# A two-layer hybrid block on one core: how eight PSUM banks are shared between score tiles and projections

## The chip, the cores and the metric

The kernel runs on one core of a Trainium2 chip. The metric is the device time of one execution in microseconds (us). The kernel before was timed three times: 2352.19, 2362.51 and 2359.31 us, median 2359.31 us. The profile was taken on a fourth execution of 2353.76 us, whose span from the first to the last instruction is 2352.0 us.

## The reference

Two blocks of two layers each work on 512 tokens of width 1024, all in fp32.

```python
# first block, twice
h = rms_norm(x, norm_g); proj = h @ w_in            # 14 pieces
y_nsa  = compressed + selected + window attention, gated   # 8 heads, causal, 512 keys
y_lru  = gated linear recurrence over a 4-tap convolution
y_conv = silu(layernorm(31-tap depthwise convolution)) @ w_pw2
x = x + concat(y * silu(z)) @ w_out
# second block, layer 0 then layer 1
x = x + mixer_ab(rms_norm(x))     # dense attention (a) and windowed attention with a sink (b), 8 heads each
x = x + cross_attention(x, mem)   # 4 heads, 256 memory tokens
x = x + swiglu(x)
x = x + mixer_cd(rms_norm(x))     # latent attention (c) and neighbourhood attention (d), 8 heads each
x = x + cross_attention(x, mem); x = x + swiglu(x); return rms_norm(x)
```

## The kernel before, in words

Activations lie transposed: eight tiles `X` of 128 channels by 512 tokens. A projection tile multiplies 128 output channels with all 512 tokens over eight tiles of `X`. Every operand of a projection is split in a high part and a low part, and each product is made by three matmuls (L410, L411, L412). So a projection tile (`dense_tile`, L443) is 24 matmuls into one PSUM bank, and VectorE or ScalarE then empties that bank. Weights come by DMA in chunks (`wr`), ScalarE makes the high part `wh` (L432), VectorE or GpSimd the low part `wl` (L365).

PSUM has eight banks. One letter each in `lay` (L301 to L305, read at L346) gives them to four uses: m projections, s scores, t transposes and statistics, o attention outputs. `lay` is `mmssstto` in the stages b (first block, both layers), a (mixer_ab) and c (mixer_cd), and `mmssttoo` in x (cross attention) and f (feed-forward). Within a letter a tile takes whichever bank of that letter is free.

Which letter a projection tile asks for is decided at L445 and L446: the letters in `spare` for the first tiles after a norm, then the letters in `dense` in turn, but only m while attention is under way (`quiet` is false from L728 until L777). The token-major projections (`tok_major`, L455) open four banks at once, by the letters in `tok`. The convolution of the first block also uses s: for each of its four channel tiles VectorE gathers 31 taps in an s bank (L895 to L899), at a low priority.

`attn` (L721) goes through pairs of query tiles. For each query tile it makes the scores of two heads, three matmuls each (L743), into two s banks; VectorE takes the row minimum (`mn`, L750 with a mask, L754 without), ScalarE the exponential into the SBUF tile `p` (L377), which frees the bank. One step later `attn_back` (L779) scales `p` (L372), transposes it on TensorE into a t bank (L798), copies it out on ScalarE (`ptt`, L805), and multiplies with the values into an o bank (L813). L745 sets which exponential a pair of score tiles has to come after:

```python
freed = len(self.exps) + nh - 1 - self.banks.count("s")
```

With two heads and three s banks that is the first exponential of the pair before; with four it is the second of the pair before that one.

The generators of a stage are stepped in the order of written strings (`FIRST`, `SECOND`, `CD_FIRST`, `CD_SECOND`), so that projections stand between the steps of attention. A scheduler then puts all instructions in order at build time, by priorities, dependences and free buffers. Each engine runs its list in that order on the chip.

Of the kernel before, what the change touches and what calls it, by code (L numbers as in the profile page):

```python
# [286 lines left out]
class Net:  # L287
# [10 lines left out]
    CD_FIRST = "0000iiiiA1rA111B2rB222C3C333D4D444D"  # L298
    CD_SECOND = "E5oE5o5F6oF6o6G7oG7o7HoH"
    CFG = {  # L300
        "b": dict(lay="mmssstto", spare="mmss", dense="m", tok="mmss", stat="t", ahead=1, pv=-200, sc="vvvv", cp=0, low=-4000, wp=0),  # L301
        "a": dict(lay="mmssstto", spare="msss", dense="ms", tok="ssmm", stat="t", ahead=1, pv=-200, sc="vvvv", cp=0, low=-4000, wp=0),
        "x": dict(lay="mmssttoo", spare="mmss", dense="ms", tok="mmss", stat="t", ahead=1, pv=-200, sc="avav", cp=0, low=-4000, wp=0),
        "f": dict(lay="mmssttoo", spare="mmss", dense="ms", tok="mmoo", stat="o", ahead=1, pv=-200, sc="avav", cp=0, low=-4000, wp=0),
        "c": dict(lay="mmssstto", spare="mmss", dense="m", tok="mmss", stat="t", ahead=1, pv=-200, sc="vvvv", cp=0, low=-4000, wp=0),  # L305
    }

    def __init__(self, tc, ctx, ap, pcols):
# [1324 lines left out]
```

## Time and profile before

| what | value |
|---|---|
| profiled execution, its span | 2353.76 us, 2352.0 us |
| runs, median | 2352.19 to 2362.51 us, 2359.31 us |
| TensorE busy | 2185.8 us, 93% |
| VectorE busy | 1464.4 us, 62% |
| ScalarE busy | 962.7 us, 41% |
| GpSimd busy | 451.4 us, 19% |
| mean granted TensorE clock | 0.971 |
| DMA | 194.73 MB, mean 83 GB/s |

Busy means that an instruction of the engine was under way. The clock is the share of full speed granted to TensorE: 1.0 is 2.4 GHz and 0.5 is 1.2 GHz. The stages lie roughly so, in us from the span's start: layer 0 of the first block up to 450 (its attention from 290), layer 1 to 885 (attention from 700), mixer_ab to 1145 (attention from 968), cross attention to 1210, feed-forward to 1600, mixer_cd to 1885, cross attention to 1960, feed-forward and the last norm to the end.

### The profile page before, as it was taken

What the parts mean: (1) busy time and instruction counts of PE and PEld (TensorE: products, weight loads), DVE (VectorE), ACT (ScalarE), POOL (GpSimd) and SP (SyncE); (2) the same over time, 40 slices, a digit from 0 to 9 for tenths busy, and PEclk for the clock granted to TensorE, in tenths of its full rate; (3) what the DMA queues carried; (4) which work ended last, traced back from release to release, by engine and by line L of the source; (5) the groups of instructions that cost most, each with busy time, mean ns of one, the idle gap of its engine ahead of it and who ended that gap; (6) DMA issues with size and microseconds to landing.
All of it is one profiled execution on the core that took longest, in us unless ns stands there. A gap on an engine that the chain in (4) does not pass through costs nothing.

```text
span 2352.0 us, 29320 instructions
## 1 busy us (share of the span) xinstructions
PE 2185.8 (93%) x11052; PEld 1731.6 (74%) x11052; DVE 1464.4 (62%) x2496; ACT 962.7 (41%) x1823; POOL 451.4 (19%) x452
## 2 busy tenths in 40 slices
PE   7999989998999989869999999999999899999998
PEld 5677856677777658546778888887767688888887
DVE  8997575499876564656665544454676655544444
ACT  4432365424235552455463322233377545322223
POOL 4434411343343133110211000001100102000002
PEclk9999999999999999989999999999999999999999
DMA  4343211133331112311323333332312132333332
GB/s 137 96 131 105 73 36 37 54 103 113 101 97 57 34 37 72 87 31 37 96 91 96 94 97 99 92 97 81 103 61 73 44 113 68 95 98 99 91 98 90
DMA packets 61436, 194.73 MB, mean 83 GB/s; under 512 B 8432, under 2 KB 10480, under 8 KB 61296
## 3 DMA queue, kind: packets, MB, share of 16 engines
q1 hardware_dynamic: 52848, 179.75, 25.0%
q10 hardware_dynamic: 8448, 13.12, 2.0%
q8 instruction: 87, 1.43, 0.3%
q14 instruction: 53, 0.43, 0.1%
HBM read 182.61 MB, written 2.10 MB: 79 GB/s over the span
## 4 chain that ended last, share of the span: by engine, by line
PE 68%; DVE 14%; DMA 7%; ACT 6%; issue 3%; POOL 2%; ACTq 1%; DVEq 0%; SPq 0%; POOLq 0%
PE ps_m L410 12%; PE ps_m L411 11%; PE ps_m L412 11%; PE ps_s L412 7%; PE ps_s L410 6%; PE ps_s L411 6%; DMA wr<-ws 4%; PE ps_s L743 4%; PE ps_o L813 3%; DVE ps_s L368 3%; PE ps_t L798 3%; ACT p L377 2%; DVE wl L365 1%; ACT wh L432 1%; ACT ptt L805 1%
## 5 line engine op out<-in xcount | busy, mean ns | idle before, releaser
L432 ACT CAST wh<-wr 128x1024 fp32r<-128x1024 f32 (+2 forms) x312 | 323.1, 1035 | 660.7 <-DMA wr<-ws 553.9
L365 DVE TENSOR_TENSOR wl<-wr,wh 128x1024 fp32r<-128x1024 f32 (+1 forms) x232 | 288.2, 1242 | 300.4 <-PE ps_m L411 140.4
L410 PE MATMUL ps_m<-xh,wh 128*128 128x512 f32 x1008 | 400.1, 397 | 17.5 <-ACT wh L432 7.9
L412 PE MATMUL ps_m<-xh,wl 128*128 128x512 f32 x1008 | 399.9, 397 | 4.0 <-POOL wl L365 2.8
L411 PE MATMUL ps_m<-xl,wh 128*128 128x512 f32 x1008 | 397.6, 394 | 2.8 <-DVE xl L368 2.8
L362 POOL TENSOR_TENSOR sq<-sq 128x512 f32<-128x512 f32 (+1 forms) x62 | 87.2, 1407 | 951.3 <-ACT sq L377 951.3
L365 POOL TENSOR_TENSOR wl<-wr,wh 128x1024 fp32r<-128x1024 f32 (+2 forms) x80 | 191.0, 2387 | 386.8 <-PE ps_m L411 220.1
L410 PEld LDWEIGHTS ps_m<-xh,wh 128*128 128x128 f32 x1008 | 191.1, 190 | 63.9 <-issue 10.3
L412 PEld LDWEIGHTS ps_m<-xh,wl 128*128 128x128 f32 x1008 | 190.7, 189 | 50.0 <-POOL wl L365 5.5
L411 PEld LDWEIGHTS ps_m<-xl,wh 128*128 128x128 f32 x1008 | 190.8, 189 | 46.5 <-DVE xl L368 4.8
L377 ACT ACTIVATE p<-ps_s,mn 128x512 f32<-128x512 f32 (+3 forms) x288 | 164.1, 576 | 78.7 <-DVE mn L750 40.9
L412 PE MATMUL ps_s<-xh,wl 128*128 128x512 f32 x480 | 188.4, 393 | 1.0 <-DVE wl L365 1.0
L410 PE MATMUL ps_s<-xh,wh 128*128 128x512 f32 x480 | 188.0, 392 | 0.0
L411 PE MATMUL ps_s<-xl,wh 128*128 128x512 f32 x480 | 187.7, 391 | 0.0
L368 DVE SCALAR_TENSOR_TENSOR ps_s<-up,params,ps_s 128x512 f32<-128x512 f32 x232 | 170.0, 750 | 2.6
L805 ACT COPY ptt<-ps_t 128x512 f32<-128x512 f32 (+3 forms) x288 | 129.2, 478 | 103.5 <-PE ps_t L798 101.4
L798 PE MATMUL ps_t<-consts,p 128*128 128x128 f32 x848 | 137.7, 294 | 23.0 <-ACT ptt L805 11.7
L798 PEld LDWEIGHTS ps_t<-consts,p 128*128 128x128 f32 x848 | 103.5, 148 | 60.8 <-ACT ptt L805 24.1
L362 DVE TENSOR_TENSOR X<-ps_m,X 128x512 f32<-128x512 f32 (+1 forms) x136 | 90.8, 671 | 58.7 <-PE ps_m L412 58.4
L412 PEld LDWEIGHTS ps_s<-xh,wl 128*128 128x128 f32 x480 | 90.7, 189 | 20.6 <-DVE wl L365 1.5
L411 PEld LDWEIGHTS ps_s<-xl,wh 128*128 128x128 f32 x480 | 90.6, 189 | 19.0
L410 PEld LDWEIGHTS ps_s<-xh,wh 128*128 128x128 f32 x480 | 90.6, 189 | 18.7 <-issue 0.2
(504 smaller groups left out, 4146.6 us busy)
## 6 DMA issues: line engine op xcount, KB each, us to landing
wr<-ws SPq DMA_DIRECT2D x318, 512.0 KB, 3.6
strip<-strips ACTq DMA_DIRECT2D x8, 480.0 KB, 4.6
wr<-ws SPq DMA_DIRECT2D x8, 384.0 KB, 3.1
X<-x SPq DMA_DIRECT2D x8, 256.0 KB, 4.8
mem<-mem SPq DMA_DIRECT2D x8, 256.0 KB, 3.0
wr<-ws SPq DMA_DIRECT2D x7, 256.0 KB, 2.7
tab<-tables SPq DMA_DIRECT2D x6, 256.0 KB, 2.8
out_dram<-ox SPq DMA_DIRECT2D x8, 128.0 KB, 1.7
```

The lines of the kernel that those rows point to most:

```text
L362: (eng or self.nc.vector).tensor_tensor(out=out, in0=a, in1=b, op=ALU.add)
L365: (eng or self.nc.vector).tensor_tensor(out=out, in0=a, in1=b, op=ALU.subtract)
L368: self.nc.vector.scalar_tensor_tensor(out=out, in0=a, scalar=s, in1=b, op0=op0, op1=op1)
L377: return self.nc.scalar.activation(out, in_, func, **k)
L410: mm(out, ah, bh, start=first, stop=False)
L411: mm(out, ah, bl, start=False, stop=False)
L412: return mm(out, al, bh, start=False, stop=last)
L432: nc.scalar.copy(wh[:, :n], wr[:, :n])
L743: run.append(lambda s=s, q=q, k=k, n=n: nc.tensor.matmul(s, q[:, sl], k[:, ks], start=n == 0, stop=n == np_ - 1))
L798: nc.tensor.transpose(t[:, j * P:(j + 1) * P], p[:, j * P:(j + 1) * P], self.con("ident"))
L805: nc.scalar.copy(dst, src)
L813: run.append(lambda n=n, j=j, a=a, b=b, hd=hd, t=t: nc.tensor.matmul(hd[2]()[:, (pr + a) * P:(pr + b) * P], hd[1](j), t[:, j, a * P:b * P] ...
```

## The change

Three of the five stages get another table of banks: b, a and c. In all three, one m bank becomes a fourth s bank. Projection tiles outside attention go to m and s in turn (b and c had m alone), the tiles after a norm go to one m and three s (`msss`), and the token-major projections to four s. The stages x and f are as they were.

```diff
-        "b": dict(lay="mmssstto", spare="mmss", dense="m", tok="mmss", stat="t", ...
-        "a": dict(lay="mmssstto", spare="msss", dense="ms", tok="ssmm", stat="t", ...
+        "b": dict(lay="msssstto", spare="msss", dense="ms", tok="ssss", stat="t", ...
+        "a": dict(lay="msssstto", spare="msss", dense="ms", tok="ssss", stat="t", ...
...
-        "c": dict(lay="mmssstto", spare="mmss", dense="m", tok="mmss", stat="t", ...
+        "c": dict(lay="msssstto", spare="msss", dense="ms", tok="ssss", stat="t", ...
```

The first place is TensorE's list in the dense attention of mixer_ab. Before, the rows are these (`ps_s` are scores, `ps_t` transposes, `ps_o` the product with the values):

```order
L798 MATMUL ps_t<-consts,p 128x128 x16
L743 MATMUL ps_s<-qh 128x512 x2
L743 MATMUL ps_s<-qh,ql 128x512 x2
L743 MATMUL ps_s<-ql,qh 128x512 x2
L813 MATMUL ps_o<-ptt,abv 64x256 x8
```

The changed program has these rows there:

```order
L813 MATMUL ps_o<-ptt,abv 64x256 x8
L798 MATMUL ps_t<-consts,p 128x128 x8
L743 MATMUL ps_s<-qh 128x512 x2
L743 MATMUL ps_s<-qh,ql 128x512 x2
L743 MATMUL ps_s<-ql,qh 128x512 x2
L798 MATMUL ps_t<-consts,p 128x128 x4
L743 MATMUL ps_s<-qh 128x512 x2
L743 MATMUL ps_s<-qh,ql 128x512 x2
L743 MATMUL ps_s<-ql,qh 128x512 x2
L798 MATMUL ps_t<-consts,p 128x128 x12
```

Sixteen transposes stood in one piece between two pairs of score tiles; now pairs of score tiles stand between pieces of eight, four and twelve transposes.

The second place is TensorE's list in the first block, layer 0, where the projections `zn` run beside the first attention (2617 and 2653 are two tiles of that projection). Before:

```order
L412 MATMUL ps_m_2617<-xh_133,wl_2621 128x512
L1157 MATMUL ps_t_2024<-consts_74,cs_2013 128x128 x2
L410 MATMUL ps_m_2617<-xh_137,wh_2620 128x512
L411 MATMUL ps_m_2617<-xl_138,wh_2620 128x512
L412 MATMUL ps_m_2617<-xh_137,wl_2621 128x512
L410 MATMUL ps_m_2653<-xh_109,wh_2656 128x512
L411 MATMUL ps_m_2653<-xl_110,wh_2656 128x512
```

Now:

```order
L412 MATMUL ps_m_2617<-xh_133,wl_2621 128x512
L410 MATMUL ps_m_2617<-xh_137,wh_2620 128x512
L411 MATMUL ps_m_2617<-xl_138,wh_2620 128x512
L412 MATMUL ps_m_2617<-xh_137,wl_2621 128x512
L410 MATMUL ps_m_2653<-xh_109,wh_2656 128x512
L411 MATMUL ps_m_2653<-xl_110,wh_2656 128x512
```

The two tiles follow each other in both lists. Before, they lie in the two m banks; now both lie in the only one, so that the first matmul of 2653 comes after VectorE has emptied 2617.

## Rows read from the trace of the kernel before

**Rows 1.** Engine busy times by stretch: PE, PEld, DVE, ACT, POOL, granted clock, DMA.

```profile
50.00:150.00 100.00, 91.37 (x415) 71.93 (x414) 99.77 (x130) 39.40 (x51) 43.10 (x30) 0.97 0.36 110
290.00:450.00 160.00, 138.62 (x807) 97.61 (x806) 102.14 (x274) 86.58 (x228) 31.16 (x24) 0.95 0.13 37
700.00:885.00 185.00, 166.59 (x933) 120.92 (x932) 113.85 (x288) 99.80 (x246) 54.03 (x37) 0.94 0.14 43
968.00:1045.00 77.00, 53.28 (x326) 32.95 (x326) 41.10 (x82) 40.81 (x95) 7.61 (x6) 0.89 0.10 26
1045.00:1145.00 100.00, 87.15 (x505) 63.10 (x506) 67.08 (x173) 56.60 (x150) 14.20 (x19) 0.93 0.17 51
1690.00:1860.00 170.00, 156.42 (x931) 113.32 (x930) 110.70 (x220) 114.47 (x247) 11.27 (x18) 1.00 0.19 58
2000.00:2300.00 300.00, 300.00 (x1313) 246.33 (x1312) 146.21 (x177) 82.04 (x94) 0.00 (x0) 1.00 0.32 95
```

**Rows 2.** TensorE's waits over the span: total us, times, longest us.

```profile
PE ps_s L743 <- ACT p L377: 33.4, 29, 5.3
PE ps_o L813 <- ACT ptt L805: 18.0, 23, 2.3
PE ps_m L410 <- DVE X L362: 14.8, 10, 3.5
PE ps_t L798 <- ACT ptt L805: 11.7, 26, 1.5
...
PE ps_t L798 <- DVE p L372: 8.7, 11, 1.6
```

**Rows 3.** The timeline of mixer_ab's attention: start us, us, engine, instruction, idle before.

```profile
1001.30 1.28 DVE L754 TENSOR_REDUCE mn<-ps_s 128x1 f32<-128x512 f32 x2
1001.39 1.14 PE L798 MATMUL ps_t<-consts,p 128*128 128x128 f32 x8 [0.59 <-ACT ptt L805]
...
1002.61 0.69 ACT L377 ACTIVATE p<-ps_s,mn 128x512 f32<-128x512 f32 x1
...
1003.29 0.68 ACT L377 ACTIVATE p<-ps_s,mn 128x512 f32<-128x512 f32 x1
1003.44 0.50 PE L743 MATMUL ps_s<-qh 64*128 64x512 f32 x2 [0.91 <-ACT p L377]
1003.78 0.40 PE L743 MATMUL ps_s<-qh,ql 64*128 64x512 f32 x2
```

**Rows 4.** The timeline where a projection waits longest for its bank.

```profile
1879.87 2.28 DVE L365 TENSOR_TENSOR wl<-wr,wh 128x1024 fp32r<-128x1024 f32 x1
1882.08 0.68 DVE L362 TENSOR_TENSOR X<-ps_m,X 128x512 f32<-128x512 f32 x1
...
1882.90 0.55 PE L410 MATMUL ps_m<-mh,wh 128*128 128x256 f32 x1 [3.50 <-DVE X L362]
```

**Rows 5.** The instructions that empty a projection's bank: ns min/median/max.

```profile
L368 DVE SCALAR_TENSOR_TENSOR z<-ps_m,rb x24: 677/690/694, 101.6 to 724.9; 128x512 f32<-128x512 f32 x24
```

**Rows 6.** TensorE's timeline in a projection beside attention.

```profile
255.03 0.39 PE L410 MATMUL ps_m<-xh,wh 128*128 128x512 f32 x1
255.26 0.39 PE L411 MATMUL ps_m<-xl,wh 128*128 128x512 f32 x1
```

**Rows 7.** The last convolution tap of each layer, and the first token-major matmuls.

```profile
215.78 0.75 DVE L368 SCALAR_TENSOR_TENSOR cy<-up,params,ps_s 128x512 f32<-128x512 f32 x1
...
220.23 0.50 PE L470 MATMUL ps_s<-wh,xh 128*128 128x280 f32 x2
...
648.89 0.75 DVE L368 SCALAR_TENSOR_TENSOR cy<-up,params,ps_s 128x512 f32<-128x512 f32 x1
...
650.82 0.50 PE L470 MATMUL ps_s<-wh,xh 128*128 128x280 f32 x2
```

More of the change, by code (lines that the diff above doesn't have):

```diff
@@ L300 @@
     CFG = {
-        "b": dict(lay="mmssstto", spare="mmss", dense="m", tok="mmss", stat="t", ahead=1, pv=-200, sc="vvvv", cp=0, low=-4000, wp=0),
-        "a": dict(lay="mmssstto", spare="msss", dense="ms", tok="ssmm", stat="t", ahead=1, pv=-200, sc="vvvv", cp=0, low=-4000, wp=0),
+        "b": dict(lay="msssstto", spare="msss", dense="ms", tok="ssss", stat="t", ahead=1, pv=-200, sc="vvvv", cp=0, low=-4000, wp=0),
+        "a": dict(lay="msssstto", spare="msss", dense="ms", tok="ssss", stat="t", ahead=1, pv=-200, sc="vvvv", cp=0, low=-4000, wp=0),
         "x": dict(lay="mmssttoo", spare="mmss", dense="ms", tok="mmss", stat="t", ahead=1, pv=-200, sc="avav", cp=0, low=-4000, wp=0),
         "f": dict(lay="mmssttoo", spare="mmss", dense="ms", tok="mmoo", stat="o", ahead=1, pv=-200, sc="avav", cp=0, low=-4000, wp=0),
-        "c": dict(lay="mmssstto", spare="mmss", dense="m", tok="mmss", stat="t", ahead=1, pv=-200, sc="vvvv", cp=0, low=-4000, wp=0),
+        "c": dict(lay="msssstto", spare="msss", dense="ms", tok="ssss", stat="t", ahead=1, pv=-200, sc="vvvv", cp=0, low=-4000, wp=0),
     }
```

## The prediction

> **What bounds the kernel now.** I began with the engines' busy times by stretch, because TensorE's 93% is a mean over stages with different limits. In the feed-forward part TensorE is busy for 300.00 of 300.00 us at full clock, and nothing there is touched. In the five stretches of attention it is busy for 138.62 of 160, 166.59 of 185, 53.28 of 77, 87.15 of 100 and 156.42 of 170 us; the worst is the dense attention of mixer_ab with 23.7 us idle [rows 1]. Together that is 90 us without TensorE. No other engine is full there: VectorE is busy for 53 to 67% and ScalarE for 53 to 67%. So TensorE is the engine that should set the pace, and what it waits for is latency, not another engine's throughput.
>
> I then read whom TensorE waits for. Four entries of the list belong to the loop of attention: score tiles that wait for an exponential, 33.4 us in 29 waits; products with the values that wait for the copy of the transposed probabilities, 18.0 us; transposes that wait for the same copy, 11.7 us; transposes that wait for the scaling, 8.7 us [rows 2]. That is 71.8 us. The timeline shows the first kind: the two row minima take 1.28 us, the exponentials 0.69 and 0.68 us, and the next score pair starts only after the first of the two, with 0.91 us of TensorE idle [rows 3]. Three banks hold one pair and a half, and so the next pair hangs on this chain.
>
> TensorE also pays by its clock: it is granted 0.95, 0.94, 0.89 and 0.93 in the first four stretches [rows 1]. Since the levels are 1.0 and 0.5, the missing share times the stretch (8 + 11 + 8.5 + 7) is at most 34.5 us of lost work.
>
> **The change part by part.** No matmul, VectorE, ScalarE or DMA instruction is added or removed. What moves is their order, and which bank a tile hangs on. I counted over TensorE's new order how much TensorE work stands between the last matmul into a bank and the next tile's first matmul in it. A dense or score matmul counts with 0.23 us, the distance of two starts [rows 6]; a transpose and a product with the values with 0.11 us.
>
> (1) Score banks. A pair needs about 2.5 us from its last matmul until both banks are free: 1.28 us of minima and 1.37 us of exponentials, partly overlapped [rows 3]. Score tiles that had less than 2.5 us of other work ahead of them were 65 in the four attention stages; in the new order they are 2. So of the 33.4 us I take off 32.
>
> (2) What follows. With the scores a pair earlier, the scaled probabilities are ready earlier, and the transposes are spread. Transposes with less than 1.5 us between two uses of a t bank fall from 70 to 19: of 11.7 us I take off 11.7 x 51/70 = 8.5. First transposes less than 4 us behind their scores fall from 26 to 0: I take off 8 of 8.7. Products with the values less than 2 us behind the last transpose fall from 46 to 21: of 18.0 I take off 18.0 x 25/46 = 9.8. Sum of (1) and (2): 58 us. From below it is bounded by nothing at all, if every wait only changes its name, from above by the 71.8 us of all four entries.
>
> (3) The one m bank. While attention is under way, a projection tile must wait until VectorE has emptied the tile before. That takes 0.69 us when VectorE is free [rows 5], some 0.8 us with the hand-overs. Projections with less than 1.0 us of cover were 4 and are 21, those with less than 2.5 us were 21 and are 54. With VectorE free each of the 17 new ones costs about 0.45 us, 8 us in all; with one VectorE instruction of 0.7 us ahead of it 1.15 us, 20 us in all. Of VectorE I know only that it is busy for about 0.6 of the time [rows 1], so the value is between the two: 14 us. The end above comes from the longest wait of this kind, 3.50 us, where a weight subtraction of 2.28 us stood ahead of the addition that frees the bank [rows 4]; behind the waiting matmul stand scores and transposes that were ready.
>
> The Trainium skill speaks against this part: Perfetto Trace Analysis, Optimizing Tensor Performance, says that independent matmul groups should go round through several PSUM banks, so that emptying one overlaps with the matmuls of the next. By that rule every projection beside attention pays; the rows have no single-bank projection to show its size, and the slower rival below is this rule at its full price.
>
> (4) The front of the two first-block layers and of mixer_cd. Outside attention projections now have five banks to go round instead of two, but the convolution's accumulators lie in the same s banks, and the token-major projection needs all four. The last tap ends at 216.5 us in layer 0, 3.7 us ahead of the first token-major matmul, and at 649.6 us in layer 1, 1.2 us ahead [rows 7]. Until now nothing hung on that. VectorE is busy for 99.77 of 100 us in the stretch from 50 to 150 us [rows 1], so the margin is real but thin. I cost it at 1 us and keep 0 to 16 us as its bounds, 8 us a layer, which is a slip by about ten taps; a gain from the wider choice of banks I put within that.
>
> (5) What takes the place of the waits. Once TensorE runs closer to full, VectorE and ScalarE rise from about 0.6 to about 0.75 of the time in these stretches, and some waits only change their name. I give back a fifth of the 58 us, 12 us.
>
> (6) The clock. Low clock stands where TensorE idles: 0.89 in the stretch with 31% idle, 1.00 in mixer_cd with 8% [rows 1]. If three quarters of the attention waits go, some of the 34.5 us comes back; I take 8 us, with 0 and 20 as ends.
>
> The Trainium skill (TensorE: Matmul & The Clock Gate, A second HAM failure mode: psum-queue depth-cycling) tells of a kernel whose many short idles between groups in cycling banks made the clock swing. By that, (3) would bring low clock back and (6) would be 0; no row of before has a single projection bank to show it.
>
> Sum: -32 -26 +14 +1 +12 -8 = -39 us. Against the profiled execution that is 2353.8 - 39 = 2314.8 us. The median of the runs before is 5.5 us above that execution, and the middle of such a difference should carry over, so I write 2317 us.
>
> **The rivals.** A: one projection bank is the new bound, and the kernel gets slower. The place is the projections beside attention in all four stages, 33 more of them with less than 2.5 us of cover. The mean wait for the addition into X was 14.8/10 = 1.5 us [rows 2]; if all 33 paid that, it is 50 us against a gain of 58 + 8, still faster by 16. From a mean of 2.0 us on it decides against the change; at 2.5 us it is 82 us and the time is 2353.8 + 16 = 2370 us, and more if the clock falls further. For it: 2.28 us subtractions on VectorE as in [rows 4] are common beside projections. Against it: VectorE has a third of its time free in these stretches.
>
> B: The waits move. Scores come early, but TensorE then waits at the transposes and the values, because VectorE and ScalarE run in order and each holds other work. Then (1) and (2) give less than half, 25 us, and with (3) the time is 2353.8 - 25 + 14 = 2343 us. For it: ScalarE is busy for 114.47 of 170 us in mixer_cd. Against it: the order gives transposes and values more distance too.
>
> C: The convolution holds banks that projections or the token-major tiles want. At 8 us a layer the time is about 2331 us. For it: 1.2 us of margin [rows 7]. Against it: the last channel's taps stand early enough in the new order.
>
> **How the numbers follow.** The forecast has 0.70, B 0.12, C 0.10, A 0.08. About 0.5%, 12 us, is what a measurement of this kernel can tell from no change. Faster by more than that holds the forecast and C: 0.80. Same holds B: 0.12. Slower is A: 0.08. The range: all gains with cheap projections and 20 us of clock give 2353.8 - 58 + 8 - 20 = 2284, which I trim to 2290; B with one more slip of the convolution reaches 2350. A is left out above.
>
> **What would show it.** Right: score waits for the exponential fall from 33.4 us to under 6, TensorE's idle in 968 to 1045 falls by half, and waits of `ps_m` for VectorE rise by 8 to 20 us. Wrong: `ps_m` waits above 50 us (A), waits for `ptt` and the scaling not lower than now (B), token-major matmuls or projections in s that wait for a tap (C). A low clock in the attention stretches as before would take (6) away.

## The result and the profile after

The changed kernel takes 2329.84 us in the median of four runs (2325.18 to 2332.87), the kernel before 2356.74 us in four runs beside it (2352.19 to 2362.51). The ratio is 0.9887, with a 95% interval from 0.9870 to 0.9904: 27 us faster, where 39 had been forecast; the time lies inside the stated range of 2290 to 2350 us. The profiled execution of the changed kernel took 2331.09 us.

The page of the profile after gives the span and the busy times:

```profile
span 2329.3 us, 29296 instructions
PE 2186.1 (94%) x11052; PEld 1739.5 (75%) x11052; DVE 1463.1 (63%) x2496; ACT 961.4 (41%) x1823; POOL 452.0 (19%) x452
```

TensorE is busy for 2186.1 us where it was busy for 2185.8. Its idle time fell from 2352.0 - 2185.8 = 166.2 us to 143.2 us, by 23.0, and the span by 22.7. So in this pair of executions the whole gain is idle time of TensorE.

The busy times of the changed kernel in the stretches that answer to [rows 1] (PE, PEld, DVE, ACT, POOL, granted clock, DMA):

```profile
50.00:150.00 100.00, 89.78 (x398) 70.74 (x397) 97.15 (x131) 39.60 (x50) 44.06 (x32) 0.95 0.34 103
290.00:450.00 160.00, 149.00 (x878) 108.53 (x878) 106.46 (x275) 91.52 (x233) 41.98 (x34) 0.98 0.17 47
690.00:875.00 185.00, 167.42 (x964) 122.32 (x963) 120.31 (x304) 99.95 (x251) 54.04 (x35) 0.96 0.15 46
970.00:1040.00 70.00, 66.28 (x474) 44.27 (x474) 58.65 (x142) 54.24 (x144) 11.55 (x8) 1.00 0.17 46
1701.00:1797.00 96.00, 84.75 (x482) 62.93 (x481) 63.41 (x120) 68.08 (x148) 7.25 (x14) 1.00 0.20 55
```

The dense attention of mixer_ab is the winner: it had 23.7 us of idle time in 77 us at a clock of 0.89, now 3.7 us in 70 us at 1.00. The two stretches do not hold the same work: the new one has 474 matmuls, the old one 326, since projections now run there too. What the stage gains is therefore read from its whole length, further down. In mixer_cd it is the other way: the 96 us from 1701 hold 11.3 us of idle time. The corresponding 96 us of the kernel before (1735 to 1831, 34 us later in the span) held 5.0.

TensorE's waits in the changed kernel, in total us, times and longest us, answer to [rows 2]:

```profile
PE ps_m L410 <- DVE X L362: 19.0, 10, 3.5
PE ps_m L410 <- DVE z L368: 18.9, 5, 5.4
PE ps_s L412 <- DVE wl L365: 13.4, 12, 2.1
PE ps_s L743 <- ACT p L377: 8.9, 14, 1.3
...
PE ps_m L410 <- DVE ga L368: 7.4, 2, 4.3
PE ps_m L410 <- ACT cf L377: 4.4, 5, 1.3
...
PE ps_o L813 <- ACT ptt L805: 3.9, 5, 2.3
...
PE ps_t L798 <- ACT ptt L805: 3.0, 7, 0.6
```

The four entries of attention were 71.8 us. They are 8.9 + 3.9 + 3.0 + 0 = 15.8 us; the wait for the scaling is gone from the list. No wait for a tap of the convolution is in it. At the head now stand projections that wait for their bank to be emptied, `z` above all, which was not in the list as a wait for `ps_m`.

The timeline of the dense attention shows the new pattern where [rows 3] showed a stop:

```profile
1003.51 0.50 PE L743 MATMUL ps_s<-qh 64*128 64x512 f32 x2
...
1003.62 0.59 ACT L805 COPY ptt<-ps_t 128x512 f32<-128x512 f32 x1 [0.42 <-PE ps_t L798]
1003.80 2.01 DVE L754 TENSOR_REDUCE mn<-ps_s 128x1 f32<-128x512 f32 x3
...
1004.52 0.69 ACT L377 ACTIVATE p<-ps_s,mn 128x512 f32<-128x512 f32 x1 [0.31 <-DVE mn L754]
```

The score pair starts with no idle time of PE ahead of it (no bracket), a microsecond before the next exponential, which belongs to the pair ahead of it in the other banks. Both pairs are in PSUM at once.

The timeline of the longest wait for `z`:

```profile
275.71 5.72 DVE L365 TENSOR_TENSOR cy<-cy,mbs 128x512 f32<-128x512 f32 x4 [5.84 <-ACT mbs L913]
...
276.29 0.39 PE L412 MATMUL ps_m<-xh,wl 128*128 128x512 f32 x1
...
276.59 2.62 POOL L365 TENSOR_TENSOR wl<-wr,wh 128x1024 fp32r<-128x1024 f32 x1 [7.53 <-PE ps_m L411]
...
281.36 0.68 DVE L368 SCALAR_TENSOR_TENSOR z<-ps_m,rb 128x512 f32<-128x512 f32 x1
...
282.09 0.80 PE L410 MATMUL ps_m<-xh,wh 128*128 128x512 f32 x1 [5.41 <-DVE z L368]
```

The projection's last matmul ends at 276.7 us. The instruction that empties its bank takes 0.68 us, as in [rows 5], but it stands in VectorE's order behind four mean subtractions of the convolution's norm, 5.72 us together, with a subtraction on GpSimd beside them. With one bank TensorE stops for 5.41 us.

The last taps and the first token-major matmuls, as in [rows 7]:

```profile
219.30 0.75 DVE L368 SCALAR_TENSOR_TENSOR cy<-up,params,ps_s 128x512 f32<-128x512 f32 x1
...
221.69 0.51 PE L470 MATMUL ps_s<-wh,xh 128*128 128x280 f32 x2
...
644.80 0.75 DVE L368 SCALAR_TENSOR_TENSOR cy<-up,params,ps_s 128x512 f32<-128x512 f32 x1
...
647.96 0.64 PE L470 MATMUL ps_s<-wh,xh 128*128 128x280 f32 x3
```

The margins are 1.6 and 2.4 us, and in the second layer the token-major projection even starts 2.9 us earlier than before.

By stretches of the whole span, the kernel before:

```profile
0.00:891.00 891.00, 799.78 (x4094) 620.63 (x4094) 664.19 (x1249) 375.06 (x762) 319.80 (x237) 0.96 0.26 81
891.00:1367.00 476.00, 434.42 (x2322) 341.66 (x2323) 274.18 (x478) 207.80 (x426) 60.13 (x95) 0.96 0.26 77
...
1596.00:1993.00 397.00, 373.41 (x1996) 290.87 (x1995) 236.68 (x402) 214.06 (x429) 52.95 (x92) 0.99 0.26 78
```

And the changed kernel:

```profile
0.00:885.00 885.00, 802.30 (x4094) 625.36 (x4094) 668.14 (x1249) 375.36 (x762) 318.71 (x238) 0.95 0.27 81
885.00:1332.00 447.00, 426.71 (x2321) 339.08 (x2322) 270.28 (x478) 207.12 (x426) 60.93 (x94) 0.97 0.28 82
...
1561.00:1970.00 409.00, 378.56 (x1996) 296.03 (x1995) 235.61 (x402) 213.21 (x430) 53.97 (x92) 0.97 0.25 75
```

The first row is the first block (up to the first matmul at L590), the second mixer_ab with its cross attention (up to the first `ps_s<-hidh`), the third mixer_cd with its cross attention (from the end of the feed-forward to the next `fg<-ps_m`). The first block gains 6 us, mixer_ab 29, mixer_cd loses 12.

The same lengths were read from the profiles of the experiments described below, each where it has the stage's old or new table and nothing else changed in it. One profile is one execution, and a segment with the same table differs between profiles, so small differences say nothing:

| segment | old table | new table |
|---|---|---|
| first block | 891.1, 895.6, 899.8 | 885.0, 883.1, 885.3, 881.9 |
| mixer_ab and cross attention | 475.9, 466.0, 472.6, 468.3 | 447.2, 445.6, 445.5, 447.8, 442.2, 441.8 |
| mixer_cd and cross attention | 397.6, 397.3, 395.4, 399.8, 399.0 | 409.7, 402.3 |

By the means of these rows the first block gains 11.7 us, mixer_ab 25.7, and mixer_cd loses 8.2. The single pair above puts too little in the first block and too much in the other two.

### The profile page after: what moved, and what is told of

Same layout as the page of the kernel before. It is cut to its first block, busy times and chain, and to the rows that moved or that the text cites. A ratio compares the mean times of both kernels' runs of the same rounds, so it can differ in the third digit from the quotient of the medians.

```text
span 2329.3 us, 29296 instructions
## 1 busy us (share of the span) xinstructions
PE 2186.1 (94%) x11052; PEld 1739.5 (75%) x11052; DVE 1463.1 (63%) x2496; ACT 961.4 (41%) x1823; POOL 452.0 (19%) x452
## 3 DMA queue, kind: packets, MB, share of 16 engines
q1 hardware_dynamic: 52848, 179.75, 25.7%
## 5 line engine op out<-in xcount | busy, mean ns | idle before, releaser
L365 DVE TENSOR_TENSOR wl<-wr,wh 128x1024 fp32r<-128x1024 f32 (+1 forms) x232 | 290.2, 1251 | 316.0 <-PE ps_m L411 143.2
L410 PE MATMUL ps_m<-xh,wh 128*128 128x512 f32 x792 | 322.8, 408 | 28.6 <-DVE z L368 12.1
L412 PE MATMUL ps_m<-xh,wl 128*128 128x512 f32 x792 | 319.2, 403 | 3.1 <-POOL wl L365 2.0
L411 PE MATMUL ps_m<-xl,wh 128*128 128x512 f32 x792 | 317.8, 401 | 2.2 <-DVE xl L368 2.2
L412 PE MATMUL ps_s<-xh,wl 128*128 128x512 f32 x696 | 274.7, 395 | 7.8 <-DVE wl L365 6.9
L410 PE MATMUL ps_s<-xh,wh 128*128 128x512 f32 x696 | 274.9, 395 | 0.0
L411 PE MATMUL ps_s<-xl,wh 128*128 128x512 f32 x696 | 272.8, 392 | 0.0
L411 PEld LDWEIGHTS ps_m<-xl,wh 128*128 128x128 f32 x792 | 153.6, 194 | 36.3 <-DVE xl L368 4.0
L412 PEld LDWEIGHTS ps_s<-xh,wl 128*128 128x128 f32 x696 | 131.6, 189 | 38.2 <-DVE wl L365 9.4
L411 PEld LDWEIGHTS ps_s<-xl,wh 128*128 128x128 f32 x696 | 132.0, 190 | 28.2 <-issue 0.4
L410 PEld LDWEIGHTS ps_s<-xh,wh 128*128 128x128 f32 x696 | 132.1, 190 | 27.5 <-issue 0.4
```

The costliest lines, as they stand in the source:

```text
L365: (eng or self.nc.vector).tensor_tensor(out=out, in0=a, in1=b, op=ALU.subtract)
L410: mm(out, ah, bh, start=first, stop=False)
L411: mm(out, ah, bl, start=False, stop=False)
L412: return mm(out, al, bh, start=False, stop=last)
```

## The experiments

**Which stage pays.** Three runs take the new row of the table in one stage alone, a fourth in b and a (e1 to e4):

```diff
# e1: "a" alone   e2: "b" alone   e3: "c" alone   e4: "b" and "a"
-        "a": dict(lay="mmssstto", spare="msss", dense="ms", tok="ssmm", ...
+        "a": dict(lay="msssstto", spare="msss", dense="ms", tok="ssss", ...
```

> The new bank table in mixer_ab (a) alone. Theory (the gain sits in mixer_ab): from the start of mixer_ab to the feed-forward the changed kernel is 29 us shorter, so this kernel is 24 to 32 us faster than before, as fast as the whole change or a little faster, and score waits for the exponential are down by about 14 us. Rival (the gain is spread over all attention stages, the landmarks only show work shifted over a border): 8 to 12 us faster.

> The new bank table in the first block (b) alone. Theory (gains in its attention are eaten by the one projection bank, landmark of its end 6 us earlier): 2 to 10 us faster than before, projections wait 18 to 20 us for z. Rival (its attention gains all of its 14.5 us of score waits and more): 15 to 25 us faster.

> The new bank table in mixer_cd (c) alone. Theory (mixer_cd loses, from its start to its end the changed kernel is 12 us longer): 8 to 14 us slower than before. Rival (the longer stretch is only work that came over the border from the feed-forward): within 4 us of before.

> The new table in b and a, the old one in c. Theory (stages add up): 30 to 40 us faster than before, 8 to 14 us faster than the whole change, and so the better kernel. Rival (nothing lost in mixer_cd): as fast as the whole change, 24 to 29 us faster than before.

Measured: a alone 2327.67 us, ratio 0.9881 [0.9843, 0.9919]; b alone 2338.96 us, 0.9948 [0.9928, 0.9968]; c alone 2359.01 us, 1.0022 [1.0005, 1.0040]; b and a 2317.97 us, 0.9841 [0.9795, 0.9888]. The three single ratios multiply to 0.9851, which their intervals join to the 0.9887 of all three. So mixer_ab carries the gain, the first block adds to it, and mixer_cd loses a little.

The theory held for a alone, 28 us faster, with the score waits down by 12.1 us to 21.3. With b alone the kernel is 12 us faster (8 to 17), between the theory's 2 to 10 and the rival's 15 to 25, and the waits for `z` are 18.8 us as expected. With c alone it is 5 us slower (1 to 9), less than the theory's 8 to 14. With b and a it is 37 us faster (26 to 48), as the theory had it, though the interval reaches into the rival's 24 to 29. Waits in mixer_cd with c alone:

```profile
PE ps_m L410 <- ACT cf L377: 4.4, 5, 1.3
PE ps_t L1314 <- ACT cvf L1396: 3.9, 2, 2.1
```

These two were 0.8 us and nothing before. ScalarE empties the bank of that projection, beside its exponentials.

**Is it the run-ahead of the scores? (e5)** The changed kernel, but a score pair comes after the same exponential as with three banks:

```diff
-                freed = len(self.exps) + nh - 1 - self.banks.count("s")
+                freed = len(self.exps) + nh - 1 - min(3, self.banks.count("s"))
```

> The changed kernel, but a pair of score tiles is tied to the same exponential as with three banks (the first of the pair before); the banks stay four. Theory (the gain comes from scores that run a pair further ahead): at least 10 us slower than the changed kernel, waits of scores for the exponential above 15 us. Rival (the free bank is enough, the tie decides nothing): within 4 us of the changed kernel, waits of scores under 10 us.

Measured: 2382.51 us, 1.0122 [1.0103, 1.0140]. The banks are those of the changed kernel, and the gain is gone and more. One wait and the dense attention of mixer_ab in this run:

```profile
PE ps_s L743 <- ACT p L377: 29.0, 26, 3.4
```

```profile
977.00:1050.00 73.00, 54.24 (x326) 35.27 (x326) 39.30 (x75) 40.41 (x92) 7.58 (x6) 0.88 0.13 36
```

The wait for the exponential is back at 29.0 us, and the four entries of attention together at 52.2 (15.8 in the changed kernel, 71.8 before). TensorE is idle for 18.8 of 73 us, and the clock is 0.88, much as in [rows 1, 2]. What pays is that a score pair no longer hangs on the pair ahead of it; the same banks without that cost 29 us against the kernel before (24 to 33).

**A second projection bank during attention (e6).** The changed kernel, with projections beside attention in m and s in turn:

```diff
-        tags = self.c["dense"] if self.quiet else "m"
+        tags = self.c["dense"]
```

> The changed kernel, but projections beside attention go to m and s in turn as outside it. Theory (the single projection bank costs what its waits say, some 20 us more than before): waits of ps_m for z, ga and cf fall by more than 15 us and the kernel is 8 to 18 us faster than the changed one. Rival (the fourth score bank is needed by the scores, and lending it gives the gain back): waits of scores for the exponential rise above 20 us, and the kernel is no faster or slower than the changed one.

Measured: 2357.78 us, 1.0010 [0.9996, 1.0025]: the gain is lost, but not where either theory had put it. The waits for `z` and `cf` are gone, as the theory had it, but without the gain. The score waits are low, 8.2 us. Two other waits have come:

```profile
PE ps_t L514 <- POOL sq L362: 17.8, 2, 9.2
...
PE ps_t L522 <- POOL rs L359: 9.0, 3, 3.4
```

The timeline at the longest of them:

```profile
272.94 2.50 DVE L365 TENSOR_TENSOR cy<-cy,mbs 128x512 f32<-128x512 f32 x4 [2.83 <-ACT mbs L913]
...
274.98 1.58 POOL L362 TENSOR_TENSOR sq<-sq 128x512 f32<-128x512 f32 x1 [5.68 <-ACT sq L377]
...
279.30 1.26 POOL L362 TENSOR_TENSOR sq<-sq 128x512 f32<-128x512 f32 x1 [0.74 <-ACT sq L377]
280.61 1.86 PE L514 MATMUL ps_t<-consts,sq 128*128 128x1 f32 x8 [9.21 <-POOL sq L362]
```

And the row of the 10 us from 280 on, with the granted clock third from the end:

```profile
280.00:290.00 10.00, 5.31 (x20) 4.13 (x20) 1.60 (x4) 2.06 (x7) 2.75 (x12) 0.50 0.00 1
```

It is the convolution's norm again. With one bank TensorE stopped in the projection `z`, whose bank stood behind the same subtractions; with two, nothing is left in its list ahead of the second statistic that could run, and it waits 9.21 us for the chain of subtractions, squares and sums. The clock stands at 0.50 behind this wait, where the kernel before has 1.00. The first block is 915.6 us long, 30.6 more than in the changed kernel: 19.3 us of it are idle time of TensorE, and 11.3 us are busy time, at a mean clock of 0.93 and not 0.95. mixer_ab is 449.5 us long, as in the changed kernel, and mixer_cd 402.6.

**Alternating outside attention, alone (e7).** The kernel before with its banks, only `dense` changed:

```diff
-        "b": dict(lay="mmssstto", spare="mmss", dense="m", ...
+        "b": dict(lay="mmssstto", spare="mmss", dense="ms", ...
# and the same in "c"
```

> The kernel before with one part of the change: projections outside attention in b and c go to m and s in turn; banks stay two m and three s. Theory (this part is worth next to nothing): within 6 us of before. Rival (it carries the gain of the first block): 8 to 14 us faster than before, as much as the new table in b alone.

Measured: 2344.49 us, 0.9955 [0.9939, 0.9972], 7 to 14 us faster, about as much as the whole new row in b. The rival was right. In its waits, `ko` and `qo` are gone (9.1 and 2.1 us before), and `X` has come down:

```profile
PE ps_s L743 <- ACT p L377: 30.0, 24, 5.5
...
PE ps_m L410 <- DVE X L362: 10.7, 5, 3.4
```

The profile does not settle where all of it lies: its first block is 888.9 us, and much of the rest of the difference to the one profile of before stands in mixer_ab (468.3 us), whose table is the old one. Against the mean of the first block with the old table, 895.5 us, 888.9 is about half of what the new table gains there. As the new row in b holds this edit too, no run shows what the fourth score bank alone is worth in the first block.

**The work that stands ahead of `z` (e8).** The version with b and a changed, and the four mean subtractions on GpSimd:

```diff
         for y in ys:
-            self.sub(y, y, mb)
+            self.sub(y, y, mb, g)
```

> The new table in b and a, the old one in c, and the four subtractions of the mean in the convolution's layer norm on GpSimd in place of VectorE. Theory (the longest projection waits, 5.4 and 5.2 us, come from the 5.7 us that these four stand ahead of the emptying of z): waits for z fall from 18.8 us by 7 to 10 us, the kernel is 4 to 10 us faster than with the new table in b and a alone. Rival (VectorE has other work there, or the layer norm becomes late): within 3 us of it or slower.

Measured: 2310.86 us, 0.9811 [0.9791, 0.9832]. Waits and timeline at the same place:

```profile
PE ps_m L410 <- DVE z L368: 4.0, 4, 1.6
```

```profile
274.55 5.04 POOL L365 TENSOR_TENSOR cy<-cy,mbs 128x512 f32<-128x512 f32 x4 [6.70 <-ACT mbs L913]
275.51 0.69 DVE L368 SCALAR_TENSOR_TENSOR z<-ps_m,rb 128x512 f32<-128x512 f32 x1 [6.84 <-PE ps_m L412]
...
276.26 0.50 PE L410 MATMUL ps_m<-xh,wh 128*128 128x512 f32 x1 [0.79 <-DVE z L368]
```

`z` is written while the subtractions run, and TensorE waits 0.79 us instead of 5.41. The waits for `z` fall from 18.8 us (b and a changed) to 4.0, by more than the 7 to 10 expected. One bank is enough where the instruction that empties it comes at once. The ratios of this run and of b and a alone come from different chips and overlap; in the pair below they do not.

The stop costs clock as well. The 10 us from 280 on, first in the changed kernel, where TensorE's wait of 5.41 us ends at 282.1, then in this run:

```profile
280.00:290.00 10.00, 7.91 (x30) 6.45 (x30) 2.33 (x3) 2.21 (x3) 3.91 (x4) 0.70 0.00 0
```

```profile
280.00:290.00 10.00, 8.25 (x36) 6.25 (x35) 1.38 (x2) 3.36 (x4) 9.26 (x6) 1.00 0.23 62
```

The granted clock is 0.70 behind the stop and 1.00 without it. In the other runs with this stop it is 0.68 (e2), 0.73 (e4) and 0.72 (e9); in e10, without it, 1.00. In the second layer, from 710 to 720 us, it is 0.70 in the changed kernel and 1.00 in e8 and e10.

**Two banks in mixer_cd alone, and both corrections (e9, e10).** In the changed kernel:

```diff
-        tags = self.c["dense"] if self.quiet else "m"
+        tags = self.c["dense"] if self.quiet or self.c is self.CFG["c"] else "m"
# e10: this, and the subtractions on GpSimd as in e8
```

> The changed kernel, but in mixer_cd (stage c) the projections beside attention go round m and a score bank again, as they do outside attention; elsewhere one bank. Theory: the 12 us that mixer_cd with the rest loses between the kernel before and the changed one (397.6 to 409.7 us) come from the one projection bank, which ScalarE empties late for c_proj (waits of ps_m for cf 4.4 us in 5, for wh 8.0 us in 3) and its followers; with two banks the segment falls to 397 to 402 us, and the time is 6 to 12 us below the changed kernel (ratio to the kernel before about 0.985). Rival: the loss lies in the front of mixer_cd and in its lower clock, not in the bank; then the segment stays at 405 to 412 us and the time is within 4 us of the changed kernel (0.987 to 0.990).

> The run before this one (all four stages changed, two projection banks beside attention in mixer_cd alone) and, beside it, the four mean subtractions ahead of z on GpSimd instead of VectorE. Theory: both corrections lie in different stretches and add up: the subtractions are worth about 7 us, as between the two runs with a and b changed (ratios 0.9841 and 0.9811), so the ratio is 0.978 to 0.982, level with or a little below the best version so far (0.9811). Rival: mixer_cd is no better with the changed table in any form, so that this stays 5 to 12 us above the version that leaves mixer_cd as before (0.983 to 0.986).

Measured, on one chip: 2319.26 us, 0.9848 [0.9825, 0.9871], and with the subtractions moved 2306.73 us, 0.9792 [0.9772, 0.9812]. In mixer_cd the waits for `cf` and `cvf` are gone in the first run (0.8 us of `cf` in the second), as the theory had it, and attention there is nearly full:

```profile
1690.00:1790.00 100.00, 96.76 (x551) 72.69 (x550) 68.23 (x131) 76.04 (x163) 7.34 (x14) 1.00 0.22 71
```

3.2 us of idle time in 100, where the changed kernel has 11.3 in 96. The segment is 403.0 us in the first of the two runs, between the theory's 397 to 402 and the rival's 405 to 412, and 398.7 in the second, against 409.7 and 402.3 with one bank. What the second bank takes away is idle time of TensorE, 30.4 us in the changed kernel and 20.9 in e9. The busy time does not come down with it: 379.2 us in the changed kernel, 382.2 in e9 at a clock of 0.97, 376.7 in e10 at 0.99. So a low clock stands there without the single bank too. The ratios put the edit at 9 us, with intervals that just touch. Of the 14.8 us between the two spans, 6.7 lie in mixer_cd; the rest lies in stages that are the same program, and is spread between executions. The subtractions are worth 13 us in this pair, with intervals apart. Their own stage shows less: the first block is 881.9 and 878.9 us long in the pair, and 885.3 (e4) and 874.4 (e8) in the other, 3 and 11 us. The last run is the fastest of all, 49.9 us below the kernel before.

## Why the prediction came out as it did

The sum had six terms. On the profiled executions it was to be -39 us and is -22.7. The medians differ by 26.9 us, so against them 12 us are missing and not 16.

**(1) and (2), -58 forecast, -56.0 measured.** The mechanism was right, and e5 shows the cause: with the same banks and the old tie 52.2 of the 71.8 us return. That the sum fits so well is partly luck. (1) brought 24.5 us where 32 were taken off, and the score waits went to 8.9 us rather than under 6; (2) brought 31.5 where 26 were, above all the products with the values, 14.1 where 9.8 were.

**(3), one m bank, +14 with 8 to 20 as bounds.** This is the term that was mis-sized. The waits of `ps_m` for the instruction that empties it went from 32.5 to 55.1 us, +22.6. In that number two effects are mixed. Of the entries that rose, `z` brings 18.9, `ga` 5.5, `X` 4.2, `cf` 3.6, `bu` 2.0 and `du` 0.6: 34.8 us. Of those that fell, `ko` brings 9.1, `qo` 2.1, `lup` 0.8 and `gb` 0.2: 12.2 us. e6, with two banks beside attention, parts them: `z`, `cf` and `du` are gone there, `ga` (7.0), `bu` (2.0) and most of `X` (17.5) are not. So the price of the one bank is 18.9 + 3.6 + 0.6 = 23.1 us, above the upper bound, and the other rises and falls nearly cancel. It was worked out as seventeen tiles with at most one instruction of 0.7 us ahead on VectorE; instead few waits were long, five for `z` with 3.8 us each on average, the two longest (5.4 and 5.2) because four instructions that had become ready together stood ahead. The 2.28 us subtraction of [rows 4] pointed the right way, and the term was still priced with 0.7 us ahead. The busy share of VectorE did not show such a queue. e8 and e10 show it: with the four instructions moved, 4.0 us of the waits for `z` are left. The term also left out the clock behind such a stop, 0.70 for about 10 us.

Two signs that were to tell the forecast from rival A both came true: the waits of `ps_m` for VectorE rose by 19.0 us, within 8 to 20, and reached 50.7, above 50. They had been 31.7 before, so the signs overlapped.

**(4), fronts and convolution, +1.** No projection or token-major matmul waits for a tap, so rival C is out. But the gain from the wider choice of banks, put within this term, is 10.6 us by the ratio of e7, with the old banks. There the sign was wrong: 1 us of cost stood where the fallen waits for `ko` and `qo` brought 11.2.

**(5), waits with another name, +12.** All other idle time rose by -23.0 + 56.0 - 22.6 = 10.4 us, for (4) and (5) together 13 were forecast. Projections in s that wait for the low part of a weight rose alone from 2.1 to 13.4 us.

**(6), the clock, -8.** In this pair it is 0: TensorE's busy time is 2185.8 and 2186.1 us, the mean clock 0.971 and 0.970. In mixer_ab it came as forecast, from 0.96 to 0.97 with 434.42 us busy before and 426.71 after. The first block and mixer_cd gave it back, 0.96 to 0.95 and 0.99 to 0.97, with 2.5 and 5.2 us more busy. But one pair does not settle a term of this size. The mean clock of the kernel before went from 0.963 to 0.973 over nineteen executions on one chip, which is more than the 0.003 that 8 us are. In the profiles of the table above, with the old table the first block has 799.8, 809.8 and 811.1 us of busy time, with the new one 801.1 to 802.3, and by the means mixer_ab comes down by 6.2 us, the first block by 5.2, and mixer_cd goes up by 2.2. That is about -9 us. So it is not shown that (6) failed, and its miss in this pair may be scatter.

What is shown is that a stop of (3) brings low clock, by the rows from 280 us in the changed kernel, e6 and e8. The Trainium skill (TensorE: Matmul & The Clock Gate, A second HAM failure mode: psum-queue depth-cycling) tells of many short idles, and the prediction drew from it that (6) would be 0; the rows here show a fall behind single waits of 5.41 and 9.21 us.

So of the missing 16.3 us of this pair, 8.6 are (3), 8.3 are (6), with that doubt, 2.0 are (1) and (2), and (4) with (5) came 2.6 better. Rival A named the right place and mechanism, and in mixer_cd alone it outweighs the gain (e3 is 0.2% slower), but its price of 2.5 us for each of 33 tiles was not reached. The 2.28 us subtractions that spoke for it are not common: the weight subtractions on VectorE before took 1.23 us in the median and 2.33 at most. Rival B is refuted by the waits of (2). What stays open is where in the span the gain of e7 lies, what the clock alone is worth, and why the first block with two banks beside attention puts no other work between the two statistics.

## What to carry to other kernels

A score pipeline that stops at its exponential gains from a bank only if the order lets the next pair start without it; check what the pair is tied to before counting banks. A use that is left with one bank costs what its emptying instruction waits behind others on its engine, so look for bursts there, such as a norm's subtractions that become ready together, and move them or keep two banks in that stage. Decide the split for each stage by itself: a second projection bank beside attention made the first block 30 us longer, and in mixer_cd it took 9.5 us of TensorE's idle time away.

## What the runs showed of the hardware

Four fp32 subtractions of 128 x 512 on VectorE took 2.50 us together when GpSimd was idle through most of them (e6, 272.94 us), and 5.72 us beside a GpSimd subtraction of 2.62 us and a sum of 1.71 us behind it (the changed kernel, 275.71 us). On GpSimd the same four took 5.04 us, 1.29 us each, and VectorE's emptying of a PSUM bank beside them kept its 0.69 us (e8). The eight subtractions of both layers in the changed kernel and in e6 (min/median/max in ns):

```profile
L365 DVE TENSOR_TENSOR cy<-cy,mbs x8: 684/1218/2837, 275.7 to 707.9; 128x512 f32<-128x512 f32 x8
```

```profile
L365 DVE TENSOR_TENSOR cy<-cy,mbs x8: 684/685/692, 272.9 to 716.4; 128x512 f32<-128x512 f32 x8
```

In each layer of the changed kernel one of the four took 2.8 us, longer than the whole GpSimd subtraction beside it (2.62 and 2.39 us); in e6 none took more than 0.69. The Trainium skill (GPSIMD Engine Reference, Specifications) says that GpSimd contends with VectorE instructions that read two inputs from SBUF; this agrees, and so does the 0.69 us of the instruction that reads one of its inputs from PSUM. It was not tried by itself.

Behind a single wait of TensorE the granted clock was low: 0.70 in the 10 us from 280 on, with a wait of 5.41 us that ends at 282.1 (the changed kernel), 0.50 with one of 9.21 us that ends at 280.6 (e6), and 1.00 at the same place in e8, where the wait was 0.79 us.
